# First mixer: products of one chain in runs on TensorE, the modulation's four at a time, low halves of weights by VectorE

## The chip, the cores and the metric

The kernel runs on one core of a Trainium2 chip. The time is the device time of one execution in microseconds (us). TensorE (PE) multiplies matrices, VectorE (DVE) and ScalarE (ACT) work on elements, GpSimd (POOL) does some of the same more slowly, and SyncE (SP) issues the transfers from memory.

## The reference, cut to what matters

Two blocks of two layers each run on 256 tokens of width 1024 in float32. Only the first layer of the first block (its "mixer") and one small vector for the second block bear on this case:

```python
h = rmsnorm(x, g)
proj = h @ even_w_in                       # 1024 x 3592
y_a = rwkv7_group(h, dh, proj[..., :1536], ...)   # 8 heads of 64
y_b = gdn_group(proj[..., 1536:], ...)            # 4 heads of 128
x = x + concat([y_a, y_b]) @ even_w_out
...
mod_l = silu(c) @ w_ada[layer] + b_ada[layer]     # 1024 x 6144, for block two
mod_c = silu(c_ctx) @ w_ada[layer] + b_ada[layer]
```

`rwkv7_group` and `gdn_group` are recurrences over the 256 tokens.

## The kernel before, in words

**Dense products.** A weight piece (128x1024 floats) is loaded by SP into `raw`. ACT copies it, rounded, into `hi`; `split_w` then forms `lo = raw - hi` (the *low half*). TensorE does three products per 128x128 tile: hi with the activation's high and low halves, lo with the high half (`mm3`; the products read `act,hi`, `act,hi`, `act,lo`). Outside the first mixer DVE forms `lo`. In the first mixer `k.weng` is GpSimd, except for the first chunk of `w_ein`. Three `hi` and three `lo` buffers rotate.

**Chains.** The recurrences are done in chunks of 64 tokens by *units*: `rwkv_unit` (four, each for two heads) and `gdn_unit` (two, each for two heads). Two units run side by side (q = 0: rwkv 0 and 1; q = 1: rwkv 2 and 3; q = 2: both gdn), each in its own buffers (a *lane*). A unit is a long chain of small products, each followed by a copy or an elementwise step on ACT or DVE that the next needs: a prelude on DVE (norms of the keys, decays), the inverse of a triangular matrix (`triangular_inverse`: ten dependent groups of 64x64 products, `Tg,Aa`, `Pg,Tt` and so on), a loop over four chunks that carries the state S (`S,WT`, `tm`, `U,tm`), the outputs (`Rr,tm`, `Rr,U`, `AR,S`) and a norm.

**The modulation** (`ada`): the vector `sv` times 1024x6144 weights, 24 MB in all, in 12 chunks of 512 columns. Of a chunk, eight products of 128 rows x 512 columns go to four strips of 32 columns of the array, four to the first start and four that add to them; ACT copies the sum out (`adat`), TensorE transposes it four times (`ct,adat`), and DVE adds it up (`adas`, `mod`). It shares TensorE with the mixer and is needed only in block two.

**Order.** Every engine works through its own list in order. A scheduler makes the lists before the run, from the dependences and from priorities that the code sets: `k.at(p)` and `k.spread` place dense work between the priorities of the chains, and `ada` gets a chunk every 65 steps. So dense products, modulation and chains are interleaved on TensorE, and the transfers of `raw` and `adaraw` on SP. A transfer whose buffer isn't free holds up those behind it on SP. The helpers give one line to many operations: L374 is every product, L377 every transpose by TensorE, L361 every ACT step, L364, L368 and L371 elementwise steps, L1454 the modulation's products.

Of the kernel before, what the change touches and what calls it, by code (L numbers as in the profile page):

```python
# [10 lines left out]
F32 = mybir.dt.float32  # L11
# [4 lines left out]
ALU = mybir.AluOpType  # L16
# [3 lines left out]
P = 128  # L20
# [8 lines left out]
def pack_w(w, kt, nc):  # L29

    K, N = w.shape
    a = w.reshape(K // (P * kt), kt, P, N // nc, nc)
    return np.ascontiguousarray(a.transpose(3, 0, 2, 1, 4)).reshape(N // nc, K // (P * kt), P, kt * nc)
# [158 lines left out]
def layout(i):  # L192
    i = {k: np.asarray(v) for k, v in i.items()}
    A = {}
    A["vec"] = vec_table(i)
    A["con"] = const_table(False)
    A["conm"] = const_table(True)
    A["xT"] = np.ascontiguousarray(i["x"][0].T.reshape(KT, P, T).transpose(1, 0, 2))
    A["pT"] = np.ascontiguousarray(i["p"][:, 0].transpose(0, 2, 1).reshape(2, 2, P, T).transpose(0, 2, 1, 3))
    w = i["even_w_in"][0]  # L200
    A["w_ein"] = pack_w(w[:, :3584], 4, 256)
    A["w_bba"] = np.ascontiguousarray(w[:, 3584:].reshape(KT, P, 8).transpose(1, 0, 2))
    A["w_lora"] = pack_w(np.concatenate([i["rwkv_w1"][0], i["rwkv_a1"][0], i["rwkv_g1"][0]], 1), 4, 256)
    A["w_lo2"] = np.ascontiguousarray(np.stack([np.concatenate([i["rwkv_w2"][0], i["rwkv_a2"][0]], 0), i["rwkv_g2"][0]], 1))
    A["w_eout"] = pack_w(i["even_w_out"][0], 4, 256)
    for l in range(2):
        A[f"w_m1{l}"] = pack_w(i["mlp_w1"][l], 4, 256)
        A[f"w_m2{l}"] = pack_w(i["mlp_w2"][l], 4, 256)
        A[f"w_pp{l}"] = pack_w(i["ple_w_proj"][l], 2, 512)
        A[f"w_pg{l}"] = pack_w(i["ple_w_gate"][l], 4, 256)  # L210
        A[f"w_up{l}"] = pack_w(i["w_up_2"][l], 4, 256)
        w = i["w_down_2"][l]
        w = np.concatenate([w, np.zeros((256, D), w.dtype)])
        A[f"w_dn{l}"] = pack_w(w, 4, 256)
    A["w_ada0"] = pack_w(i["w_ada_2"][0], 2, 512)
    A["w_ada1"] = np.ascontiguousarray(i["w_ada_2"][1].T).reshape(48, P, D)
    A["crow"] = np.ascontiguousarray(np.broadcast_to(np.stack([i["c_2"][0], i["c_ctx_2"]]), (P, 2, D)))
    A["w_qkv"] = pack_w(i["attn_w_qkv"][0], 4, 256)
    A["w_ao"] = pack_w(i["attn_w_out"][0], 4, 256)
    A["w_ie"] = pack_w(i["w_in_e_2"][0], 4, 256)  # L220
    A["w_oe"] = pack_w(i["w_out_e_2"][0], 4, 256)
    A["w_io"] = pack_w(i["w_in_o_2"][0], 4, 256)
    A["w_oo"] = pack_w(i["w_out_o_2"][0], 4, 256)
    A["ctxT"] = np.ascontiguousarray(i["ctx_2"][0].T.reshape(KT, P, T).transpose(1, 0, 2))
    A["abias"] = attn_bias(i["attn_rel_bias"][0])
    A["nbias"] = na_bias(i["na_rpb_2"][0])
    A["fwd"], A["inv"], A["hyz"], A["hydec"] = dft_tables()
    A["hyw1"] = i["hy_w1_2"][0]
    A["hyw23"] = np.ascontiguousarray(np.stack([i["hy_w2_2"][0], i["hy_w3_2"][0]], 1))
    A["hyw4"] = i["hy_w4_2"][0]  # L230
    return A
# [41 lines left out]
class K:  # L273
    def __init__(self, nc, tc, A, es):
        self.nc, self.tc, self.A, self.es = nc, tc, A, es
        self.cp = self.pool("const", 1)
        self.wraw = self.pool("wraw", 4)
        self.whi = self.pool("whi", 3)
        self.wlo = self.pool("wlo", 3)
        self.psG = self.pool("psG", 1, PSUM)  # L280
        self.sms = [self.pool(f"small{i}", 2) for i in range(3)]
        self.ap = [self.pool("acts0", 1), None]
        self.modp = self.pool("modp", 1)
        self.pse = None
        self.weng = nc.vector
        self.slots = None
        self.later, self.slow = [], []

    def pool(self, name, bufs, space=None, es=None, side=None):
# [81 lines left out]
        (eng or self.nc.vector).scalar_tensor_tensor(out=out, in0=a, scalar=s, in1=b, op0=op0, op1=op1)  # L371

    def mm(self, out, lhsT, rhs, start=True, stop=True):
        self.nc.tensor.matmul(out=out, lhsT=lhsT, rhs=rhs, start=start, stop=stop)  # L374

    def tr(self, out, in_):
        self.nc.tensor.transpose(out=out, in_=in_, identity=self.ident)  # L377

    def vec(self, name, j=0, n=1):
        o = VEC[name] + j  # L380
# [24 lines left out]
    def split_w(self, raw, n, kt):  # L405
        hi = self.whi.tile([P, 1024], F32R, name="hi")
        lo = self.wlo.tile([P, 1024], F32R, name="lo")
        self.act(hi[:, :n], raw[:, :n])
        self.tt(lo[:, :n], raw[:, :n], hi[:, :n].bitcast(F32), ALU.subtract, eng=self.weng)
        return (hi[:, :n].rearrange("p (k n) -> p k n", k=kt), lo[:, :n].rearrange("p (k n) -> p k n", k=kt))  # L410

    def mm3(self, ps, w, x, first, last):
# [558 lines left out]
def layer0_mixer(k, x, bg, ple):  # L971

    nc, A = k.nc, k.A
    es = ExitStack()
# [14 lines left out]
    lanes = [lane(1), lane(2)]  # L989
# [10 lines left out]
    for c in range(4):  # L1000
        xc = x[:, 2 * c:2 * c + 2]
        for e in range(2):
            j = 2 * c + e
# [15 lines left out]
    rst = big.tile([P, T], F32, name="rst")  # L1019
    nc.gpsimd.memset(rst, 1.0)  # L1020
    nc.gpsimd.memset(rst.rearrange("p (c t) -> p c t", c=4)[:, :, 0:1], 0.0)
    rkv = {}
# [12 lines left out]
    lt = big.tile([P, 2, T], F32, name="lt")  # L1035
# [25 lines left out]

    bg()
    lo2 = []
    weng, k.weng = k.weng, nc.vector
    g = k.trickle(norm(), NPACE0, 1)
    for _ in k.chunk("w_ein", 2, [4, 4], [H], lambda *a: (k.finish(g), evac_rkv(*a))):
        pass
    k.weng = weng
    nc.sync.dma_start(out=k.cm, in_=A["conm"])
    lora()  # L1070
    for i in range(2):
# [8 lines left out]
    kq, raws = {}, {}  # L1080
# [32 lines left out]
    G = None  # L1113
    ya, yo = [], []
    L = UNIT
    for q in range(3):
        p = t0 + q * L
        if q == 0:
            dense((3, 1, 5), evac_rkv, p, p + L * 0.9)
        elif q == 1:  # L1120
            dense((6, 8, 10, 7, 9, 11), evac_gdn, p, p + L)
            k.at(p + L // 2)
            G = gdn_gates(k, gp, H, wbb, rb)
        else:
            dense((12, 13), evac_gdn, p, p + L * 0.5)
            yh, yl = y = k.acts(0)
            for m in range(4):
                k.split_act(yh[:, m, :T], yl[:, m, :T], ya[m])
            with k.spread(p + EO[0] * L, p + EO[1] * L, 16):
                for _ in out_proj1(k, "w_eout", y, x, [(0, 0, 4)]):  # L1130
                    pass
            k.at(p + PL * L)
            for _ in ple.products(lambda: k.psD.tile([P, 2, T], F32, name="psx")):
                pass
        for u in range(2):
            k.at(p + u * OFS)
            k.lane(1 + u)
            if q < 2:
                m = 2 * q + u
                ya.append(rwkv_unit(k, m, rkv[0, m], rkv[1, m], rkv[2, m], lt, lo2, rst, *lanes[u]))  # L1140
            else:
                yo.append(gdn_unit(k, u, G, [kq[2 * u], kq[2 * u + 1]], raws[1, u], raws[2, u], *lanes[u]))
            k.lane(0)
    k.at(t0 + 3 * L)
    for u in range(2):
# [286 lines left out]
def ada(k, l, es, step, ofs=0):  # L1432


    nc = k.nc
    w = k.pool("adaw", 2 if l else 3, es=es, side="right")
    o = k.pool("adao", 1, es=es, side="right")
    mod = k.mods[l]
    sv = o.tile([P, KT, 32], F32, name="sv")
    k.at(k.now + ofs)  # L1440
    p = k.now
    nc.gpsimd.memset(sv, 0.0)
    k.act(sv[:, :, 0], k.vec("c", 0, 8), AF.Silu)
    k.act(sv[:, :, 1], k.vec("cctx", 0, 8), AF.Silu)
    for c in range(12):
        k.tc.cur_priority = p + step * c
        ps = k.psG.tile([P, 512], F32, name="psg")
        for pi in range(4):
            raw = w.tile([P, 2, 512], F32, name="adaraw")
            nc.sync.dma_start(out=raw, in_=k.A[f"w_ada{l}"][c, pi].rearrange("p (j n) -> p j n", j=2))  # L1450
            for j in range(2):
                kk = 2 * pi + j
                q = 32 * (kk % 4)
                nc.tensor.matmul(out=ps[q:q + 32], lhsT=sv[:, kk], rhs=raw[:, j], start=kk < 4, stop=kk >= 4, tile_position=(0, q))  # L1454
        t = o.tile([P, 512], F32, name="adat")
        k.act(t, ps)
        ps = k.psG.tile([P, 4, P], F32, name="psg")
        for m in range(4):
            k.tr(ps[:, m], t[:, m * P:(m + 1) * P])
        a = o.tile([P, 4, 2], F32, name="adas")  # L1460
        nc.vector.tensor_reduce(out=a, in_=ps.rearrange("p m (q r) -> p m r q", q=4)[:, :, 0:2], op=ALU.add, axis=AX.X)
        k.tt(mod[:, 4 * c:4 * c + 4], a, k.vec(f"bada{l}", 4 * c, 4)[:, :, None].to_broadcast([P, 4, 2]), ALU.add)
    for j in (8, 32):
        k.ts(mod[:, j:j + 8], mod[:, j:j + 8], 1.0, ALU.add)
    k.tc.cur_priority = p - ofs
# [748 lines left out]
def program(nc, tc, A, out):  # L2214
    with ExitStack() as es:
        k = K(nc, tc, A, es)
# [4 lines left out]
        k.plep = k.pool("plep", 1, es=es1, side="right")  # L2221
        ple = [Ple(k, l) for l in range(2)]
        with ExitStack() as esa:
            k.weng = nc.gpsimd
            y = layer0_mixer(k, x, lambda: ada(k, 0, esa, STEP, OFS0), ple[0])
            k.weng = nc.vector
        k.banks(3, 4)
        k.ap[1] = k.pool("acts1", 1)
        k.stp = stp = k.pool("stp", 1)
# [46 lines left out]
```

## Time and profile before

| | |
|---|---|
| median of 3 runs | 1981.81 us (1980.93 to 1985.22) |
| the profiled execution | 1984.02 us, span of its instructions 1982.2 us |
| first mixer, from the span's start to the end of its last chain | about 388 us |
| TensorE busy over the span | 1904.9 us (96%) |
| DVE / ACT / GpSimd busy | 1382.6 / 911.6 / 161.3 us |

TensorE counts as busy from a product's start to its modelled end, and products overlap; an isolated product is busy two or three times as long as it holds up the next. So a busy share near 100% does not say that the engine could take nothing more. Times in the profile are from the span's start.

### The profile page before, as it was taken

What the parts mean: (1) busy time and instruction counts of PE and PEld (TensorE: products, weight loads), DVE (VectorE), ACT (ScalarE), POOL (GpSimd) and SP (SyncE); (2) the same over time, 40 slices, a digit from 0 to 9 for tenths busy, and PEclk for the clock granted to TensorE, in tenths of its full rate; (3) what the DMA queues carried; (4) which work ended last, traced back from release to release, by engine and by line L of the source; (5) the groups of instructions that cost most, each with busy time, mean ns of one, the idle gap of its engine ahead of it and who ended that gap; (6) DMA issues with size and microseconds to landing.
All of it is one profiled execution on the core that took longest, in us unless ns stands there. A gap on an engine that the chain in (4) does not pass through costs nothing.

```text
span 1982.2 us, 36281 instructions
## 1 busy us (share of the span) xinstructions
PE 1904.9 (96%) x14540; PEld 1682.0 (85%) x14540; DVE 1382.6 (70%) x2838; ACT 911.6 (46%) x1527; POOL 161.3 (8%) x211
## 2 busy tenths in 40 slices
PE   7999999999999999999999998899999999899998
PEld 4665668899999889999998887678888898788998
DVE  6544627586558878676876789859877578888664
ACT  4313224455446665545465555433213354465443
POOL 3412214100000100000001100000000000200000
PEclk9999978999999999999999999899999999999999
DMA  6544312255655446556422113235774254324553
GB/s 242 205 165 149 97 57 75 67 186 184 194 192 199 154 130 206 185 193 195 154 81 62 44 38 104 90 128 197 239 267 157 86 172 158 107 77 161 189 182 127
DMA packets 84401, 292.14 MB, mean 147 GB/s; under 512 B 9639, under 2 KB 11528, under 8 KB 83976
## 3 DMA queue, kind: packets, MB, share of 16 engines
q1 hardware_dynamic: 84232, 289.82, 44.3%
q8 instruction: 114, 1.87, 0.4%
q14 instruction: 55, 0.45, 0.1%
HBM read 288.73 MB, written 1.05 MB: 146 GB/s over the span
## 4 chain that ended last, share of the span: by engine, by line
PE 81%; DVE 13%; ACT 2%; issue 2%; POOL 1%; DMA 0%; ACTq 0%; SPq 0%; DVEq 0%
PE psx L374 75%; PE psg L1454 3%; DVE lo L364 3%; PE psx L377 2%; PE psg L374 1%; ACT hi L361 1%; POOL qb L364 1%; DVE mt L371 1%; DVE act L371 0%; DVE qx L364 0%; DVE hu L371 0%; ACT act L361 0%; DVE qms L1309 0%; DVE act L364 0%; DVE nt L364 0%
## 5 line engine op out<-in xcount | busy, mean ns | idle before, releaser
L374 PE MATMUL psx<-act,hi 128*128 128x256 f32 (+1 forms) x3872 | 830.2, 309 | 23.4 <-ACT hi L361 11.4
L361 ACT ACTIVATE hi<-raw 128x1024 fp32r<-128x1024 f32 (+1 forms) x440 | 453.6, 1032 | 652.0 <-PE psx L374 459.1
L374 PEld LDWEIGHTS psx<-act,hi 128*128 128x128 f32 x3872 | 633.9, 192 | 92.3 <-issue 32.4
L364 DVE TENSOR_TENSOR lo<-raw,hi 128x1024 fp32r<-128x1024 f32 (+1 forms) x406 | 482.0, 1189 | 265.8 <-ACT hi L361 264.2
L374 PE MATMUL psx<-act,lo 128*128 128x256 f32 (+1 forms) x1936 | 596.4, 308 | 4.1 <-DVE lo L364 3.6
L374 PEld LDWEIGHTS psx<-act,lo 128*128 128x128 f32 x1936 | 371.7, 192 | 42.1 <-issue 18.8
L374 PE MATMUL psx<-hi,act 128*128 128x256 f32 x1280 | 242.2, 289 | 2.7 <-ACT act L361 1.5
L374 PEld LDWEIGHTS psx<-hi,act 128*128 128x128 f32 x1280 | 198.8, 190 | 11.2 <-issue 7.0
L374 PE MATMUL psx<-lo,act 128*128 128x256 f32 x640 | 180.8, 283 | 1.2 <-DVE lo L364 1.2
L374 PE MATMUL psx<-fh,hi 128*128 128x256 f32 (+2 forms) x528 | 162.3, 308 | 4.9 <-DVE xc L371 4.9
L374 PE MATMUL psx<-fh,lo 128*128 128x256 f32 (+2 forms) x528 | 162.4, 308 | 1.3 <-DVE lo L364 1.3
L374 PE MATMUL psx<-fl,hi 128*128 128x256 f32 (+2 forms) x528 | 161.7, 306 | 0.0
L374 PE MATMUL psx<-hh,hi 128*128 128x256 f32 x512 | 142.4, 278 | 0.0
L374 PE MATMUL psx<-hlo,hi 128*128 128x256 f32 x512 | 142.2, 278 | 0.0
L374 PE MATMUL psx<-hh,lo 128*128 128x256 f32 x512 | 142.2, 278 | 0.0
L374 PEld LDWEIGHTS psx<-lo,act 128*128 128x128 f32 x640 | 121.5, 190 | 1.4 <-DVE lo L364 1.4
L374 PEld LDWEIGHTS psx<-fh,hi 128*128 128x128 f32 x528 | 101.3, 192 | 10.9 <-issue 6.0
L374 PEld LDWEIGHTS psx<-fh,lo 128*128 128x128 f32 x528 | 101.3, 192 | 8.0 <-DVE lo L364 2.1
L374 PEld LDWEIGHTS psx<-fl,hi 128*128 128x128 f32 x528 | 101.3, 192 | 4.5
L364 POOL TENSOR_TENSOR lo<-raw,hi 128x1024 fp32r<-128x1024 f32 x34 | 81.4, 2396 | 223.6 <-ACT hi L361 167.7
L1484 DVE CUSTOM_DVE_ANT_0 adat<-adaraw,adac 128x1024 f32<-128x1024 f32 x64 | 78.3, 1223 | 28.1 <-DMA adaraw<-in_w_ada 27.1
L374 PEld LDWEIGHTS psx<-hlo,hi 128*128 128x128 f32 x512 | 96.9, 189 | 0.0
(499 smaller groups left out, 2501.6 us busy)
## 6 DMA issues: line engine op xcount, KB each, us to landing
raw<-in_w_m SPq DMA_DIRECT2D x128, 512.0 KB, 3.4
adaraw<-in_w_ada SPq DMA_DIRECT2D x96, 512.0 KB, 4.2
raw<-in_w_up SPq DMA_DIRECT2D x92, 512.0 KB, 3.3
raw<-in_w_dn SPq DMA_DIRECT2D x48, 512.0 KB, 3.4
raw<-in_w_ein SPq DMA_DIRECT2D x28, 512.0 KB, 4.7
raw<-in_w_ie SPq DMA_DIRECT2D x28, 512.0 KB, 3.4
raw<-in_w_qkv SPq DMA_DIRECT2D x24, 512.0 KB, 3.5
raw<-in_w_io SPq DMA_DIRECT2D x18, 512.0 KB, 3.7
```

The lines of the kernel that those rows point to most:

```text
L361: self.nc.scalar.activation(out=out, in_=in_, func=func, **kw)
L364: (eng or self.nc.vector).tensor_tensor(out=out, in0=a, in1=b, op=op)
L371: (eng or self.nc.vector).scalar_tensor_tensor(out=out, in0=a, scalar=s, in1=b, op0=op0, op1=op1)
L374: self.nc.tensor.matmul(out=out, lhsT=lhsT, rhs=rhs, start=start, stop=stop)
L377: self.nc.tensor.transpose(out=out, in_=in_, identity=self.ident)
L1454: nc.tensor.matmul(out=ps[q:q + 32], lhsT=sv[:, kk], rhs=raw[:, j], start=kk < 4, stop=kk >= 4, tile_position=(0, q))
L1484: nc.vector.tensor_tensor_reduce(out=t, in0=raw, in1=row[:, s], scale=1.0, scalar=0.0, op0=ALU.mult, op1=ALU.add, accum_out=mod[:, j, s:s ...
```

## The change

Five edits, all in the first mixer or in what it shares memory with.

- `mm` and `tr` go through a new `pe`. Inside `with k.chains()` a product that is traced directly behind another one (nothing else traced between them) is ordered behind the first of its run on TensorE and gets priority 0, so that the run's products follow as soon as they can. Both kinds of unit are traced in `chains()`.
- A modulation piece is now 1024 KB instead of 512 KB (`pack_w(..., 4, 512)`), with two buffers in place of three; four products of a piece are a run of `chains()`.
- `lo` is formed by DVE everywhere (`weng` goes).
- `dynamic_dma_scratch_size=1024` gives room in the on-chip memory for the larger pieces.

```diff
-    A["w_ada0"] = pack_w(i["w_ada_2"][0], 2, 512)
+    A["w_ada0"] = pack_w(i["w_ada_2"][0], 4, 512)
...
+    def pe(self, emit):
+
+        if not self.runs:
+            emit()
+            return
+        traced = self.nc.cur_bb.bb.instructions
+        if self.head is not None and traced[-1] is self.last:
+            p = self.now
+            self.at(0)
+            with self.tc.issue_after(self.head):
+                self.last = emit().ins
+            self.at(p)
+        else:
+            self.head = self.last = emit().ins
...
-        self.tt(lo[:, :n], raw[:, :n], hi[:, :n].bitcast(F32), ALU.subtract, eng=self.weng)
+        self.tt(lo[:, :n], raw[:, :n], hi[:, :n].bitcast(F32), ALU.subtract)
...
-    w = k.pool("adaw", 2 if l else 3, es=es, side="right")
+    w = k.pool("adaw", 2, es=es, side="right")
...
-        for pi in range(4):
-            raw = w.tile([P, 2, 512], F32, name="adaraw")
-            nc.sync.dma_start(out=raw, in_=k.A[f"w_ada{l}"][c, pi].rearrange("p (j n) -> p j n", j=2))
-            for j in range(2):
-                kk = 2 * pi + j
-                q = 32 * (kk % 4)
-                nc.tensor.matmul(out=ps[q:q + 32], lhsT=sv[:, kk], rhs=raw[:, j], start=kk < 4, stop=kk >= 4, tile_position=(0, q))
+        for pi in range(2):
+            raw = w.tile([P, 4, 512], F32, name="adaraw")
+            nc.sync.dma_start(out=raw, in_=k.A[f"w_ada{l}"][c, pi].rearrange("p (j n) -> p j n", j=4))
+            with k.chains():
+                for j in range(4):
+                    q = 32 * j
+                    k.pe(lambda: nc.tensor.matmul(out=ps[q:q + 32], lhsT=sv[:, 4 * pi + j], rhs=raw[:, j], start=pi == 0, stop=pi == 1, tile_position=(0, q)))
...
-            k.weng = nc.gpsimd
             y = layer0_mixer(k, x, lambda: ada(k, 0, esa, STEP, OFS0), ple[0])
-            k.weng = nc.vector
...
-    nc = bacc.Bacc("TRN2", target_bir_lowering=False, num_devices=1)
+    nc = bacc.Bacc("TRN2", target_bir_lowering=False, num_devices=1, dynamic_dma_scratch_size=1024)
```

What moves in the engines' lists: over the first mixer the 96 modulation products stand in 69 separate runs before and in 24 runs of four after. The dense products (`act,hi`, `act,lo`, `act,wbh`, `act,wbl`, `ph`, `plo`) stand in 166 stretches between other products before, in 119 after; the chains' products in 130 stretches before, 98 after. On DVE 36 subtractions are added, and on POOL 36 go. From the first layer's MLP on, TensorE's list is the same in both, down to its end (10,963 of 13,197 entries).

TensorE, before, in the opening of the mixer: dense products of `w_ein`, with the modulation's products (`adaraw,sv`) between them.

```order
L1454 MATMUL psg<-adaraw,sv 32x512
L374 MATMUL psx<-act,hi 128x256 x2
L1454 MATMUL psg<-adaraw,sv 32x512
L374 MATMUL psx<-act,lo 128x256
L1454 MATMUL psg<-adaraw,sv 32x512
L374 MATMUL psx<-act,hi 128x256 x2
L1454 MATMUL psg<-adaraw,sv 32x512
L374 MATMUL psx<-act,lo 128x256
L1454 MATMUL psg<-adaraw,sv 32x512
```

Five products of the modulation stand apart there, each between dense ones. After, there are two runs in the same opening, of this form:

```order
L374 MATMUL psx<-act,hi 128x256 x2
L1474 MATMUL psg<-adaraw,sv 32x512 x4
L374 MATMUL psx<-act,lo 128x256
L374 MATMUL psx<-act,hi 128x256 x2
L374 MATMUL psx<-act,lo 128x256
```

TensorE, before, in the triangular inverse of rwkv units 0 and 1: each x16 is one product group of both lanes (eight blocks each).

```order
L374 MATMUL psx<-Tg,Aa 64x64 x16
L1454 MATMUL psg<-adaraw,sv 32x512
L374 MATMUL psx<-Pg,Tt 64x64 x16
L1454 MATMUL psg<-adaraw,sv 32x512 x4
L374 MATMUL psx<-Tg,Aa 64x64 x16
L1454 MATMUL psg<-adaraw,sv 32x512
L374 MATMUL psx<-act,lo 128x256
L374 MATMUL psx<-act,hi 128x256 x2
L374 MATMUL psx<-act,lo 128x256
L374 MATMUL psx<-Pg,Tt 64x64 x16
L1454 MATMUL psg<-adaraw,sv 32x512 x2
```

After, the same place:

```order
L374 MATMUL psx<-Tg,Aa 64x64 x16
L374 MATMUL psx<-Pg,Tt 64x64 x16
L374 MATMUL psx<-act,hi 128x256
L374 MATMUL psx<-Tg,Aa 64x64 x8
L374 MATMUL psx<-act,hi 128x256
L1474 MATMUL psg<-adaraw,sv 32x512 x4
L374 MATMUL psx<-Tg,Aa 64x64 x8
L374 MATMUL psx<-Pg,Tt 64x64 x16
L374 MATMUL psx<-act,lo 128x256
L374 MATMUL psx<-Tg,Aa 64x64 x8
```

In the whole of this inverse there were ten runs of the modulation, and one is left. Fewer dense products stand between the groups, and the lanes' blocks of eight come one lane after the other.

DVE, after, while the first norm (`nt`, `rbp`) is computed that the first evacuation (`zsh`) waits for; before, no `lo` stands there:

```order
L368 TENSOR_SCALAR nt<-psx 128x256
L364 TENSOR_TENSOR lo<-raw,hi 128x1024
L368 TENSOR_SCALAR rbp<-nt 128x256
L364 TENSOR_TENSOR lo<-wb,hi 128x1024
L364 TENSOR_TENSOR nt<-rbp 128x256
L364 TENSOR_TENSOR raw<-raw,wb 128x1024
L364 TENSOR_TENSOR nt<-nt 128x256
L371 SCALAR_TENSOR_TENSOR nt<-nt 128x256
L371 SCALAR_TENSOR_TENSOR rbp<-nt,rbp 128x256
L364 TENSOR_TENSOR lo<-raw,hi 128x1024
L364 TENSOR_TENSOR nt<-rbp 128x256
L364 TENSOR_TENSOR lo<-wb,hi 128x1024
```

The four low halves have come from POOL's list into the middle of this norm. Of the 36 that come to DVE, 11 stand ahead of the first unit's DVE steps and 25 among those of the units.

## Rows read from the trace of the kernel before

**Rows 1.** Stretches: length, busy PE, PEld, DVE, ACT, POOL; clock, DMA share, GB/s

```profile
0.00:34.00 34.00, 20.89 (x102) 14.06 (x103) 24.44 (x32) 15.67 (x24) 11.57 (x17) 1.00 0.72 259
34.00:68.00 34.00, 34.00 (x204) 22.14 (x202) 10.10 (x15) 10.62 (x13) 14.71 (x8) 1.00 0.62 219
68.00:175.00 107.00, 100.29 (x944) 65.12 (x947) 56.11 (x149) 30.30 (x63) 24.57 (x22) 0.97 0.47 161
175.00:302.00 127.00, 123.01 (x979) 79.49 (x972) 58.37 (x169) 38.30 (x77) 24.79 (x20) 0.87 0.29 94
302.00:388.00 86.00, 82.17 (x901) 74.28 (x900) 56.37 (x145) 38.46 (x65) 30.43 (x19) 0.96 0.21 69
139.00:151.00 12.00, 12.00 (x127) 9.18 (x127) 6.71 (x19) 1.44 (x6) 2.44 (x3) 1.00 0.19 63
247.00:272.00 25.00, 25.00 (x91) 17.09 (x90) 5.26 (x22) 9.37 (x19) 3.63 (x2) 0.52 0.12 43
```

**Rows 2.** Waits on the chain that ended last, 0 to 388 us

```profile
by line: PE psx L374 52.6%; PE psg L1454 15.1%; issue 5.0%; PE psx L377 1.7%; DVE nt L364 1.4%; DMA adaraw<-in_w_ada 1.4%; DVE nrs L371 1.3%; PE psg L377 1.3%; DVE mod L364 1.2%; ACT act L361 1.1%; DVE dsh L371 1.0%; ACT hi L361 1.0%; DVE r
...
20.82 2.09 DVE raw L364
...
30.34 0.43 DVE nt L371
...
292.90 2.06 DVE ntm L364
```

**Rows 3.** Groups of instructions, 0 to 388 us

```profile
L1454 PE MATMUL psg<-adaraw,sv 128*32 128x512 f32 x192 | 76.2, 616 | 1.9 <-DMA adaraw<-in_w_ada 1.9
...
L364 POOL TENSOR_TENSOR lo<-raw,hi 128x1024 fp32r<-128x1024 f32 x34 | 81.4, 2396 | 223.6 <-ACT hi L361 167.7 <-PE psx L374 29.4 <-ACT Pg L361 26.4
...
L364 DVE TENSOR_TENSOR lo<-raw,hi 128x1024 fp32r<-128x1024 f32 x4 | 4.9, 1220 | 1.0 <-ACT hi L361 1.0
```

**Rows 4.** TensorE in order of time, in the opening: start, length, products

```profile
35.00 0.40 PE L374 MATMUL psx<-act,hi 128*128 128x256 f32 x2
35.24 0.28 PE L374 MATMUL psx<-act,lo 128*128 128x256 f32 x1
...
42.94 0.28 PE L374 MATMUL psx<-act,hi 128*128 128x256 f32 x1
43.15 1.04 PE L1454 MATMUL psg<-adaraw,sv 128*32 128x512 f32 x2
44.12 0.38 PE L374 MATMUL psx<-act,hi 128*128 128x256 f32 x1
44.44 1.04 PE L1454 MATMUL psg<-adaraw,sv 128*32 128x512 f32 x2
```

**Rows 5.** TensorE in order of time, in the two rwkv inverses

```profile
112.22 1.20 PE L374 MATMUL psx<-Tg,Aa 64*64 64x64 f32 x32
...
115.45 1.06 PE L1454 MATMUL psg<-adaraw,sv 128*32 128x512 f32 x8
116.44 1.20 PE L374 MATMUL psx<-Tg,Aa 64*64 64x64 f32 x32
...
138.59 0.66 PE L377 MATMUL psg<-ct,adat 128*128 128x128 f32 x4
...
232.27 1.20 PE L374 MATMUL psx<-Tg,Aa 64*64 64x64 f32 x32
...
241.37 1.25 PE L374 MATMUL psx<-Tt,Pg 64*64 64x64 f32 x32
```

**Rows 6.** Stretches as in rows 1, the modulation's products (L1454) alone: PE, PEld

```profile
34.00:68.00 34.00, 12.59 (x36) 1.69 (x36) 1.00 0.62 219
```

**Rows 7.** POOL and DVE in order of time, 139 to 142 us

```profile
139.51 2.36 POOL L364 TENSOR_TENSOR lo<-raw,hi 128x1024 fp32r<-128x1024 f32 x1 [15.20 <-PE psx L374]
139.55 2.33 DVE L364 TENSOR_TENSOR mod<-adas,vt 128x8 f32<-128x8 f32 x1
...
```

**Rows 8.** What SP's queue waited for, 0 to 388 us: total, times, longest

```profile
SPq L1450 <- PE psg L1454: 142.6, 35, 16.0
```

More of the change, by code (lines that the diff above doesn't have):

```diff
@@ L284, in __init__ @@
         self.pse = None
-        self.weng = nc.vector
         self.slots = None
+        self.runs, self.head = False, None
         self.later, self.slow = [], []
@@ L373, in mm, with chains @@
     def mm(self, out, lhsT, rhs, start=True, stop=True):
-        self.nc.tensor.matmul(out=out, lhsT=lhsT, rhs=rhs, start=start, stop=stop)
+        self.pe(lambda: self.nc.tensor.matmul(out=out, lhsT=lhsT, rhs=rhs, start=start, stop=stop))
     def tr(self, out, in_):
-        self.nc.tensor.transpose(out=out, in_=in_, identity=self.ident)
+        self.pe(lambda: self.nc.tensor.transpose(out=out, in_=in_, identity=self.ident))
+    def pe(self, emit):
[11 more added lines that the diff above has]
+            self.head = self.last = emit().ins
+    @contextmanager
+    def chains(self):
+        self.runs = True
+        yield
+        self.runs, self.head = False, None
     def vec(self, name, j=0, n=1):
@@ L1063, in layer0_mixer @@
     lo2 = []
-    weng, k.weng = k.weng, nc.vector
     g = k.trickle(norm(), NPACE0, 1)
@@ L1067, in layer0_mixer @@
         pass
-    k.weng = weng
     nc.sync.dma_start(out=k.cm, in_=A["conm"])
@@ L1137, in layer0_mixer @@
             k.lane(1 + u)
[L1138 to L1142, printed above, removed]
+            with k.chains():
+                if q < 2:
+                    m = 2 * q + u
+                    ya.append(rwkv_unit(k, m, rkv[0, m], rkv[1, m], rkv[2, m], lt, lo2, rst, *lanes[u]))
+                else:
+                    yo.append(gdn_unit(k, u, G, [kq[2 * u], kq[2 * u + 1]], raws[1, u], raws[2, u], *lanes[u]))
             k.lane(0)
@@ L1447, in ada @@
         ps = k.psG.tile([P, 512], F32, name="psg")
-        for pi in range(4):
-            raw = w.tile([P, 2, 512], F32, name="adaraw")
-            nc.sync.dma_start(out=raw, in_=k.A[f"w_ada{l}"][c, pi].rearrange("p (j n) -> p j n", j=2))
-            for j in range(2):
-                kk = 2 * pi + j
-                q = 32 * (kk % 4)
-                nc.tensor.matmul(out=ps[q:q + 32], lhsT=sv[:, kk], rhs=raw[:, j], start=kk < 4, stop=kk >= 4, tile_position=(0, q))
+        for pi in range(2):
+            raw = w.tile([P, 4, 512], F32, name="adaraw")
+            nc.sync.dma_start(out=raw, in_=k.A[f"w_ada{l}"][c, pi].rearrange("p (j n) -> p j n", j=4))
+            with k.chains():
+                for j in range(4):
+                    q = 32 * j
+                    k.pe(lambda: nc.tensor.matmul(out=ps[q:q + 32], lhsT=sv[:, 4 * pi + j], rhs=raw[:, j], start=pi == 0, stop=pi == 1, tile_position=(0, q)))
         t = o.tile([P, 512], F32, name="adat")
```

## The prediction

> **What bounds the kernel now.** I read the changed lists first: from the first MLP on, TensorE's list is the same in both kernels, so everything happens in the first mixer, the first 388 us of the span. Then the busy time by stage [rows 1]. TensorE is nominally full in every stage after the first, but the clearest sign is elsewhere: in 34 to 68 us it takes 34.00 of 34 us while DVE has 10.10 and ACT 10.62. In the unit stages (68 to 175, 175 to 302, 302 to 388) DVE is at 52, 46 and 66%. So TensorE is contended, and no other engine is full. Third, the chain of waits over the mixer [rows 2]: 52.6% of it are TensorE's other products, 15.1% the modulation's, which is 0.151 × 388 = 58.6 us. The groups of instructions [rows 3] give the modulation 76.2 us of TensorE in all (two records per product, so 192 for 96). About 77% of its time is therefore on the path: the mixer waits for a vector that nobody needs before block two.
>
> **What a modulation run costs.** One product alone holds TensorE from 43.15 to 44.12, 0.97 us [rows 4]. Four that follow each other (the x8 row) hold it from 115.45 to 116.44, 0.99 us [rows 5]: they lie in different strips of 32 columns and run at the same time. The price is per run, not per product. 69 runs took 76.2 us, 1.10 each, a few of them at the lower clock. 24 runs of four at 1.0 take 24 us. TensorE is freed of 52 us; the part on the path shrinks from 58.6 to 0.77 × 24 = 18.5. **Term 1: -40 us.** Bounds: -52 if all of it was in the way; -17 if it counts only where I can see it directly. That is, first, an inverse: ten dependent products took 26.4 us (112.22 to 138.59) with ten runs among them, but five took 9.1 us (232.27 to 241.37) with none [rows 5]; at that pace ten take 18.2, so the first inverse gives 8 us. Second, 34 to 68 us, where TensorE alone is full: the modulation has 12.59 us there for 18 products [rows 6]; the same products in runs of four take 4.5, and 8 go.
>
> The Trainium skill speaks for less here: in "TensorE: Matmul & The Clock Gate", Part 3, a packing of three column strips (M=32, N=512) is listed with a speedup of 2.38, not 3. An estimate by that share gives a run of four about 1.24 us, 24 runs 30 us, and a gain some 4 us smaller. The x8 row, 0.99 us against 0.97, decides for the full factor of four, and I keep it.
>
> **Fewer changes of shape.** Two dense products hold TensorE from 35.00 to 35.24, 0.12 each; one dense product between two modulation runs holds it from 44.12 to 44.44, 0.32; one ahead of a run 0.21 (42.94 to 43.15) [rows 4]. Every entry from dense work into tiled work thus costs 0.1 to 0.2 us beside the products. The dense stretches fall from 166 to 119: 47 × 0.2 = 9.4, of which 0.77 on the path. **Term 2: -7 us** (0 to -9; 0 if the chains, not TensorE, set the pace there).
>
> **Low halves from POOL to DVE.** POOL took 2.40 us for one, DVE takes 1.22 [rows 3]. While POOL does one, DVE can stand: `mod`, 128x8 elements, took 2.33 us from 139.55, beside a POOL subtraction of 2.36 from 139.51 [rows 7]. On the chain of waits there are eleven DVE pieces of 2.06 to 2.90 us, the first at 20.82, the last at 292.90, where a step of 128x256 at 30.34 takes 0.43 [rows 2]. Taken together about 20 us of the path are such standing, and it ends. In exchange DVE gets 36 × 1.22 = 44 us. Eleven come ahead of the units: most of these fall where DVE has 10.10 of 34 us busy [rows 1] and cost nothing there (without that cover, up to 13 us). 25 stand among the units' steps, 30.5 us. A subtraction delays a chain when it stands in front of a step that is ready; I take DVE's busy share over 68 to 388, (56.11 + 58.37 + 56.37) / 320 = 53%, as the share that does: 16 us. **Term 3: -4 us** (-20 if all hide in DVE's waits; +10 if all 25 lie on the path).
>
> **Coarser transfers.** Two buffers of 1024 KB replace three of 512 KB, in the same 24 MB. SP already stood 142.6 us in 35 waits with a modulation load at its head [rows 8], 4.1 us each, and weight loads behind it. There are now 24 loads and the lists put several runs in close pairs, so both buffers come free together and 2 MB have to land before the next pair. In the opening 34 × (259 + 219) = 16.25 MB landed by 68 us [rows 1]; at 259 GB/s that needs 62.7 us, whereas terms 1 and 2 would put that point at about 58. **Term 4: +4 us** (0 to +12; the upper end if every second pair waits 2 us).
>
> **The clock.** From 247 to 272 us the granted share was 0.52, nearly all at 1.2 GHz, and the state loop that took 12 us in 139 to 151 at a share of 1.00 took 25 [rows 1]. Ahead of the drop TensorE had the small products of an inverse with a few dense ones between [rows 5]. In the new lists the first inverse looks more like that, with one or two dense products between the groups in place of modulation. A drop could come in another stage (+13) or two (+26), or that one could go (-13). **Term 5: +2 us.**
>
> The rest is free: the larger `adaw` pool and the smaller scratch are room only, and `adat`'s copies, transposes and sums are as many as before. POOL, which loses 36 subtractions, keeps its fills, `Dm`, `yn`, `kb` and `kd`; nothing waits on it more than now.
>
> **Sum.** -40 - 7 - 4 + 4 + 2 = -45 us. The profiled execution took 1984.0 us, so 1939.0; it lay 2.2 us above the median of the three runs, which gives **1937 us**. The gain should be spread as some 10 us in the opening, 15 to 20 in each rwkv stage and little in the gdn stage, where there is no modulation.
>
> **The rivals.**
> *Chains take over.* The freed TensorE time turns into idle: a product's successor waits for ACT and DVE anyway. For it: the eleven long DVE pieces and the 5.0% of the path that nothing explains. Against: only 58.6 of 76.2 us need be on the path for term 1, and the two inverses show the difference directly. Term 1 falls to its lower bound, -17, which makes the sum -22: 1960, or 1973 with one more clock drop.
>
> *More than that.* Nearly all of TensorE's 52 + 9 us is returned and the long half-speed stretch goes as well: 1981.8 - 61 - 13 + 4 = 1912; anything below 1920 counts here.
>
> *DVE's list blocks the chains: slower.* A low half in DVE's list waits until ACT has made `hi`, and ACT for its load; on POOL that wait cost nobody anything, and it was 167.7 us in all [rows 3]. On DVE, every chain step listed behind it stands too. Without term 3 the other terms give 41 us, with the 20 of standing 61; 25 subtractions use that up at 2.4 us each, their own 1.22 included. If they take 3.2 us on average, the time is 1981.8 - 61 + 80 = 2001. Against: POOL's waits were long because it had nothing else to do, and the list puts few subtractions inside the inverses. The Trainium skill ("TensorE: Matmul & The Clock Gate", Architectural detail) calls ACT's and DVE's queues strict first-in first-out, which is this rival's premise; no row here shows how long such waits on DVE would be.
>
> *The change doesn't do what it says.* The four products of a run wait one by one, or late 1 MB pieces hold TensorE for as long as the runs save: within 4 us of 1982. Against: one piece holds all four operands.
>
> **How the numbers follow.** My forecast, a gain of 25 to 62 us (1920 to 1957): 0.62. More: 0.12. Chains take over or clock drops (1957 to 1978): 0.15. No change: 0.04. Slower: 0.07. A measurement here tells 0.2%, 4 us, from no change. So faster 0.89, same 0.04, slower 0.07. The range 1908 to 1966 leaves out the slower and unchanged cases, some 0.07 of the smaller gains and 0.03 below. The forecast's own range is 1920 to 1957.
>
> **What the changed profile would show.** Right: the modulation's products at 24 to 27 us busy and under 7% of the mixer's chain of waits; no DVE piece of 128x256 above 2 us; the first inverse at 18 to 21 us; the last `og` transposes near 338 us instead of 383; nothing different after the mixer but its start. Wrong: TensorE idle ahead of chain products, released by DVE, with a `lo` just ahead on DVE; waits of TensorE for `adaraw`; a granted share below 0.8 in the first rwkv stage; POOL-like long pieces on DVE still there. A gain near 20 us would mean that term 1's share of the path was wrong, one near 70 that the chains had waited for TensorE nearly always.

## The result and the profile after

| | before | after |
|---|---|---|
| median | 1981.37 us (1977.54 to 1985.22, 4 runs) | 1896.94 us (1895.3 to 1898.74, 4 runs) |
| the profiled execution | 1984.02 us | 1898.16 us, span 1896.2 us |
| granted clock over the span | 0.977 | 0.985 |

The ratio is 0.9563, with an interval of 0.953 to 0.9597. The change gains about 87 us. 45 were forecast, and the time lies below the range. Of the 85.9 us between the two profiled executions, 82.5 are gone by the end of the first mixer: its last `og` transpose starts at 301.4 us instead of 383.9.

The mixer in stages of after (length, busy PE, PEld, DVE, ACT, POOL; clock, DMA share, GB/s), to be laid beside [rows 1]. The last two rows are most of the state loops of the two rwkv stages.

```profile
0.00:54.00 54.00, 40.91 (x305) 34.12 (x305) 34.34 (x58) 25.68 (x38) 1.24 (x15) 1.00 0.83 309
54.00:124.00 70.00, 69.81 (x868) 52.05 (x868) 46.92 (x143) 24.94 (x54) 5.73 (x13) 1.00 0.52 195
124.00:201.00 77.00, 76.54 (x923) 58.12 (x922) 52.03 (x157) 31.18 (x63) 5.54 (x11) 1.00 0.45 163
201.00:304.00 103.00, 100.73 (x1032) 89.58 (x1030) 70.83 (x184) 50.03 (x84) 7.68 (x11) 0.93 0.24 78
101.00:109.00 8.00, 8.00 (x61) 5.99 (x59) 4.38 (x16) 1.06 (x1) 0.00 (x0) 1.00 0.01 3
178.00:188.00 10.00, 10.00 (x87) 8.02 (x87) 4.45 (x15) 1.63 (x3) 0.00 (x0) 1.00 0.17 52
```

By the first and last instructions of each stage, the opening shrinks from 68.0 to 54.0 us, the first rwkv stage from 105.5 to 69.8, the second from 128.3 to 77.0, and the gdn stage grows from 82.1 to 100.7. POOL's column is nearly empty, and the 1.2 GHz stretch of the second rwkv stage is gone. From its first `S,WT` product to its last, the state loop of the second rwkv stage took 22.7 us before; after it takes 10.1, at a share of 1.00. (Only part of that is the clock, as term 5 below shows.)

The chain of waits of after, 0 to 304 us: first the shares by line (as [rows 2]), then every low half of DVE on it.

```profile
by line: PE psx L374 72.2%; PE psg L1474 6.6%; DVE lo L364 3.0%; DMA adaraw<-in_w_ada 2.4%; PE psx L377 2.1%; PE psg L377 1.9%; issue 1.4%; ACT act L361 1.3%; DMA x<-in_xT 1.2%; ACT hi L361 1.0%; DVE kbe L364 0.5%; ACT Pg L361 0.5%; DVE Tt 
...
10.98 1.24 DVE lo L364
...
20.95 1.13 DVE lo L364
...
22.29 1.13 DVE lo L364
...
26.14 1.19 DVE lo L364
...
37.84 1.23 DVE lo L364
...
39.51 7.30 DMA adaraw<-in_w_ada
...
245.88 1.98 DVE lo L364
249.53 1.13 DVE lo L364
```

TensorE's products are now 72.2% of the path instead of 52.6%, and the modulation is down from 15.1% to 6.6%. Of DVE's 39 low halves (37 from `raw`, two from `wb`) seven are on the path, 9.0 us in all: five in the opening (5.9 us; the first of them was DVE's before, too) and two among the units (3.1 us). One wait for a modulation load stands out, 7.30 us at 39.51.

Groups of after over the same stretch (busy, mean ns | idle before), to be laid beside [rows 3]:

```profile
L364 DVE TENSOR_TENSOR lo<-raw,hi 128x1024 fp32r<-128x1024 f32 x37 | 45.9, 1242 | 13.8 <-ACT hi L361 5.4 <-PE psx L374 5.2 <-DMA strm<-in_ctxT 2.7
...
L1474 PE MATMUL psg<-adaraw,sv 128*32 128x512 f32 x192 | 25.6, 604 | 0.4 <-DMA adaraw<-in_w_ada 0.4
```

The modulation takes 25.6 us instead of 76.2. SP's waits with a modulation load at its head, in the view of waits [rows 8]:

```profile
SPq L1470 <- PE psg L1474: 48.2, 15, 8.7
```

TensorE of after in order of time, the first inverse: first, one of the modulation's runs in it, and last rows (as [rows 5]).

```profile
82.31 1.15 PE L374 MATMUL psx<-Tg,Aa 64*64 64x64 f32 x32
83.47 1.15 PE L374 MATMUL psx<-Pg,Tt 64*64 64x64 f32 x32
...
85.79 1.07 PE L1474 MATMUL psg<-adaraw,sv 128*32 128x512 f32 x8
86.79 0.68 PE L374 MATMUL psx<-Tg,Aa 64*64 64x64 f32 x16
...
96.54 1.33 PE L374 MATMUL psx<-Tt,Pg 64*64 64x64 f32 x32
97.80 0.39 PE L374 MATMUL psx<-act,hi 128*128 128x256 f32 x1
```

The ten dependent product groups take 15.5 us (82.31 to 97.80), against 26.4 before.

### The profile page after: what moved, and what is told of

Same layout as the page of the kernel before. It is cut to its first block, busy times and chain, and to the rows that moved or that the text cites. A ratio compares the mean times of both kernels' runs of the same rounds, so it can differ in the third digit from the quotient of the medians.

```text
span 1896.2 us, 36237 instructions
## 1 busy us (share of the span) xinstructions
PE 1831.4 (97%) x14540; PEld 1660.7 (88%) x14540; DVE 1383.3 (73%) x2874; ACT 911.2 (48%) x1526; POOL 75.4 (4%) x175
## 4 chain that ended last, share of the span: by engine, by line
PE 86%; DVE 9%; ACT 2%; issue 1%; POOL 1%; DMA 1%; SPq 0%; ACTq 0%; DVEq 0%
PE psx L374 81%; DVE lo L364 3%; PE psx L377 2%; PE psg L1474 1%; PE psg L374 1%; ACT hi L361 1%; POOL qb L364 1%; DVE qx L364 0%; DVE mt L371 0%; DMA adaraw<-in_w_ada 0%; ACT act L361 0%; DVE act L371 0%; DVE act L364 0%; PE psg L377 0%; DVE qms L1329 0%
## 5 line engine op out<-in xcount | busy, mean ns | idle before, releaser
L374 PE MATMUL psx<-act,hi 128*128 128x256 f32 (+1 forms) x3872 | 821.0, 307 | 24.4 <-ACT hi L361 11.0
L364 DVE TENSOR_TENSOR lo<-raw,hi 128x1024 fp32r<-128x1024 f32 (+1 forms) x440 | 524.4, 1194 | 283.1 <-ACT hi L361 273.3
L374 PEld LDWEIGHTS psx<-hh,hi 128*128 128x128 f32 x512 | 96.1, 188 | 0.0
L374 PEld LDWEIGHTS psx<-hh,lo 128*128 128x128 f32 x512 | 96.1, 188 | 0.0
```

Source lines behind the costliest of these rows:

```text
L364: (eng or self.nc.vector).tensor_tensor(out=out, in0=a, in1=b, op=op)
L374: self.pe(lambda: self.nc.tensor.matmul(out=out, lhsT=lhsT, rhs=rhs, start=start, stop=stop))
```

## The experiments

The change has three parts that can be switched apart: the modulation's runs of four, the low halves on DVE, and the runs inside the units. The first three kernels do one part alone, three others leave one out. Each line below gives the median of the kernel and of the kernel before beside it; a gain is given by the ratio. The scheduler makes the lists anew for each kernel, so none of them differs from another in its edit alone: the modulation, not touched in e2 and e5, stands in 69 runs before, 66 in e2 and 59 in e5. `dynamic_dma_scratch_size` is changed in e1, e3 and e5 as well, and no run has that edit by itself.

**e1, the modulation alone.** Before, with `pe`, the 1 MB pieces and `chains()` around a piece; the units are not in `chains()`.

```diff
-    w = k.pool("adaw", 2 if l else 3, es=es, side="right")
+    w = k.pool("adaw", 2, es=es, side="right")
...
+            with k.chains():
+                for j in range(4):
```

> The kernel before with the modulation's edit alone: 1 MB pieces, runs of four (24 runs instead of 69), the low halves still on POOL, no runs in the units. Theory A (the modulation's hold on TensorE was the larger half of the 85 us, and nearly all of its 52 us came back): 50 us faster, about 1932. Theory B (the rest came because DVE no longer stands beside POOL, and so TensorE is fed steadily and keeps its clock; the modulation gave no more than the 40 us of the prediction's first term): 30 to 40 us faster, about 1945, with half-speed stretches of 40 us or more left in the first 388 us.

1945.76 us (1944.28 to 1958.72) against 1986.47; ratio 0.9808 [0.9757, 0.9859], about 38 us. Its second state loop ran at 1.2 GHz even longer than before's did:

```profile
210.00:254.00 44.00, 44.00 (x197) 30.26 (x196) 9.37 (x34) 12.32 (x25) 2.44 (x2) 0.50 0.13 42
```

**e2, the low halves alone.** Before, without GpSimd for `lo`.

```diff
-            k.weng = nc.gpsimd
             y = layer0_mixer(k, x, lambda: ada(k, 0, esa, STEP, OFS0), ple[0])
-            k.weng = nc.vector
```

> The kernel before with the low halves by DVE and nothing else. Theory A: within 8 us of before, as the prediction's third term (-4) has it. Theory B: 25 to 40 us faster, about 1950, since the eleven long DVE pieces on the chain of waits go and half-speed stretches with them.

1955.86 us (1949.73 to 1957.88) against 1986.47; ratio 0.984 [0.9796, 0.9883], about 32 us where the prediction gave this part 4.

**e3, the runs in the units alone.**

```diff
-            if q < 2:
+            with k.chains():
+                if q < 2:
```

> The kernel before with runs in the units alone (rwkv_unit and gdn_unit inside chains()), modulation and low halves as before. Both theories: a small gain, 5 to 12 us (the prediction's second term, -7); over 20 us would be a third cause that neither has: that a chain's products standing together shorten the chains themselves.

1967.49 us (1964.67 to 1970.75) against 1986.47; ratio 0.9899 [0.9849, 0.9948], about 20 us. The three single gains sum to 90 us, about what all of them give together (87).

**e4, no modulation at all.** Before, without the modulation's loads, products, copies, transposes and sums; the vector for block two is a constant.

```diff
-    for c in range(12):
...
+    nc.gpsimd.memset(mod, 0.1)
```

> The kernel before without the modulation of block two's first layer: its loads, products, copies, transposes and sums are left out and its result is filled with a constant. It bounds what the modulation costs in all. By its share of the chain of waits 59 us come back (about 1922), by its busy time with the transposes 85. Theory A: 70 us or more. Theory B: 45 to 60.

1930.6 us (1923.02 to 1935.49) against 1986.47; ratio 0.9714 [0.9666, 0.9762], about 57 us. That is what the whole modulation cost by itself. Theory A falls: e1 with 38 us, e2 with 32 and e4 with 57 all lie where theory B put them. e3 lies above the 5 to 12 us that both had, near the 20 from which a third cause was to be looked for.

**e5, both engines.** What makes e2 worth 32 us? Either DVE no longer stands beside POOL's subtractions (theory S), or `lo` is there earlier, since DVE forms it in 1.2 us and POOL in 2.4 (theory L). Here DVE forms `lo`, and POOL does the same 36 subtractions into a tile that nobody reads.

```diff
-        self.tt(lo[:, :n], raw[:, :n], hi[:, :n].bitcast(F32), ALU.subtract, eng=self.weng)
+        self.tt(lo[:, :n], raw[:, :n], hi[:, :n].bitcast(F32), ALU.subtract)
+        if self.weng is self.nc.gpsimd:
+            self.tt(self.spare[:, :n], raw[:, :n], hi[:, :n].bitcast(F32), ALU.subtract, eng=self.weng)
```

> The kernel before with the low halves by DVE, as in the DVE-only run, and POOL still doing its 36 subtractions of the same operands, into a tile that nobody reads. Theory S (DVE stands while POOL subtracts; that standing was the cost): the 30 us of the DVE-only run are gone, the time is that of before or up to 20 us more. Theory L (the low half is ready 1.2 us earlier after hi, and that was the gain): 20 us or more faster than before still.

1986.94 us (1982.25 to 1990.54, 10 runs) against 1983.52; ratio 1.0005 [0.9974, 1.0036]. All of e2's gain is lost again, so L falls. Groups of e5's mixer, then the same of e2, and last the sum `mod` in the mixer of before:

```profile
L364 POOL TENSOR_TENSOR spare<-raw,hi 128x1024 f32<-128x1024 f32 x34 | 94.9, 2791 | 165.1 <-ACT hi L361 98.1 <-issue 55.6 <-DVE x L364 9.5
L364 DVE TENSOR_TENSOR lo<-raw,hi 128x1024 fp32r<-128x1024 f32 x39 | 60.8, 1560 | 31.6 <-ACT hi L361 31.6
...
L368 DVE TENSOR_SCALAR dsh<-zsh,vt 128x256 f32<-128x256 f32 x12 | 6.0, 525 | 0.0
L364 DVE TENSOR_TENSOR mod<-adas,vt 128x8 f32<-128x8 f32 x12 | 6.0, 497 | 0.1
```

```profile
L364 DVE TENSOR_TENSOR lo<-raw,hi 128x1024 fp32r<-128x1024 f32 x39 | 47.4, 1221 | 32.8 <-ACT hi L361 22.1 <-ACT Z L361 4.0 <-ACT Pg L361 2.9
...
L368 DVE TENSOR_SCALAR dsh<-zsh,vt 128x256 f32<-128x256 f32 x12 | 4.5, 387 | 0.0
L364 DVE TENSOR_TENSOR mod<-adas,vt 128x8 f32<-128x8 f32 x12 | 1.9, 162 | 0.1
```

```profile
L364 DVE TENSOR_TENSOR mod<-adas,vt 128x8 f32<-128x8 f32 x12 | 10.5, 878 | 0.2
```

With POOL at work DVE's own subtraction takes 1560 ns instead of 1221, and the 128x8 sum 497 instead of 162. POOL also holds `raw` and `hi` longer in e5 than in e2, and the lists differ; neither is separated in the 31 us between them.

**e6, e7, e8: after with one part undone.** e6 forms `lo` on POOL again, e7 has the old modulation, e8 no runs in the units.

```diff
+            k.weng = nc.gpsimd
             y = layer0_mixer(k, x, lambda: ada(k, 0, esa, STEP, OFS0), ple[0])
+            k.weng = nc.vector
```

```diff
-    A["w_ada0"] = pack_w(i["w_ada_2"][0], 4, 512)
+    A["w_ada0"] = pack_w(i["w_ada_2"][0], 2, 512)
...
-    w = k.pool("adaw", 2, es=es, side="right")
+    w = k.pool("adaw", 2 if l else 3, es=es, side="right")
```

```diff
-            with k.chains():
+            if True:
                 if q < 2:
```

> The changed kernel with the low halves on POOL again, as before; modulation in runs and runs in the units stay. If the three edits add up: 1897 + 31 = 1928. If they share one pool of freed time: at most 15 us above the changed kernel, 1912. Theory S also expects long DVE pieces of 2 us and more back on the chain of waits.

> The changed kernel with the modulation as before: 512 KB pieces, three buffers, no runs of four. If the edits add up: 1897 + 39 = 1936. If they share the freed time: 1915 or less.

> The changed kernel without runs in the units; modulation in runs and low halves by DVE stay. If the edits add up: 1897 + 19 = 1916. If they share the freed time: within 8 us of the changed kernel, 1897 to 1905.

Against 1983.52: e6 1933.64 us (ratio 0.9744 [0.9685, 0.9804]), e7 1944.47 (0.9801 [0.9741, 0.9861]), e8 1916.81 (0.9664 [0.9597, 0.973]). Taken from after's 1896.94, the low halves are worth 37 us there, the modulation 48, the unit runs 20. So the gains don't share one pool of freed time, which would have put e6 at 1912 or less and e7 at 1915 or less. In e6 theory S expected long DVE pieces back on the chain of waits, and they are: eleven single pieces of 2.10 to 2.49 us, where after's path has no DVE piece of 2 us or more. First the shares of e6's path, then three of the pieces:

```profile
by line: PE psx L375 56.6%; PE psg L1477 6.1%; DVE dsh L372 5.3%; PE psx L378 2.6%; issue 2.2%; DMA raw<-in_w_ein 1.9%; DVE nt L365 1.7%; PE psg L378 1.6%; DVE bt L365 1.3%; DVE dsh L369 1.1%; DVE zsh L365 1.0%; DVE tmp L369 0.9%; DVE ntm L
...
20.66 2.37 DVE raw L365
...
188.33 2.29 DVE dsh L372
...
315.16 2.25 DVE oms L372
```

e8, without the unit runs, has the 1.2 GHz stretch in its second state loop again:

```profile
198.00:222.00 24.00, 24.00 (x143) 19.64 (x135) 6.16 (x22) 7.55 (x18) 0.10 (x1) 0.51 0.11 33
```

**e9, big pieces without runs of four.** After, with `chains()` around a piece taken away.

```diff
-            with k.chains():
+            if True:
                 for j in range(4):
```

> The changed kernel with 1 MB modulation pieces, but without runs of four: the four products of a piece are placed singly (67 runs in the list, as in the kernel before). Theory: only the runs matter, the piece size nothing, so this is as slow as with the old modulation (1944): 1937 to 1950. If the larger pieces gave part of the gain: 1930 or less.

1945.25 us (1940.0 to 1954.32) against 1984.82; ratio 0.9795 [0.9758, 0.9832], the time of e7. Without runs of four, the size of the pieces is worth nothing either way. Its modulation, in the groups of its mixer:

```profile
L1474 PE MATMUL psg<-adaraw,sv 128*32 128x512 f32 x192 | 70.2, 605 | 0.0
```

**e10, e11, e12: the gdn stage.** Why is it 19 us longer in after? Runs in the gdn units might hold dense products back (theory G; e10 takes those runs out), or too much dense work is left for the last stage (theory D; e11 puts one chunk a stage earlier, e12 shortens the planned stage from 320 steps to 260).

```diff
+            if q < 2:
+                with k.chains():
...
+            else:
+                if True:
```

```diff
-            dense((3, 1, 5), evac_rkv, p, p + L * 0.9)
+            dense((3, 1, 5), evac_rkv, p, p + L * 0.7)
+            dense((6,), evac_gdn, p + L * 0.7, p + L * 0.95)
...
-            dense((6, 8, 10, 7, 9, 11), evac_gdn, p, p + L)
+            dense((8, 10, 7, 9, 11), evac_gdn, p, p + L)
```

```diff
-UNIT = 320
+UNIT = 260
```

> The changed kernel with runs in the four rwkv units and none in the two gdn units. The gdn stage was 18 us longer in the changed kernel's trace than before. Theory D (dense work that the faster rwkv units ran ahead of is done there, 175 dense products instead of 78 between the last rwkv product and the first gdn product): within 6 us of the changed kernel, 1892 to 1903. Theory G (the runs themselves hold up the gdn units): 10 us or more faster, 1887 or less.

> The changed kernel with one of the six dense chunks of the second unit stage (chunk 6) given priorities in the first, so that 103 instead of 175 dense products are left between the last rwkv product and the first gdn product. Theory D: TensorE is idle or waits in the first rwkv stage often enough to take part of these 72 products (8.6 us at 0.12): 3 to 9 us faster, about 1891. If TensorE is the bound in every stage alike: within 3 us of the changed kernel.

> The changed kernel with UNIT at 260 instead of 320, the distance in priorities between the unit stages, so that dense work stands closer in the stages (145 dense products left between the last rwkv product and the first gdn product). Theory D: 0 to 5 us faster. If TensorE is the bound in every stage alike: within 3 us of the changed kernel.

Against 1984.82: e10 1907.74 us (1906.92 to 1908.59; ratio 0.96 [0.9571, 0.9629]), e11 1896.96 (0.9549 [0.9522, 0.9576]), e12 1899.61 (0.9557 [0.953, 0.9584]). G falls: without their runs the gdn units are slower, and only they. The stages of e10 are those of after up to 201 us, and the last is 11 us longer:

```profile
54.00:124.00 70.00, 69.80 (x868) 52.03 (x868) 46.88 (x143) 24.95 (x54) 5.73 (x13) 1.00 0.52 196
124.00:201.00 77.00, 76.28 (x920) 57.91 (x919) 51.84 (x156) 31.19 (x63) 5.48 (x11) 1.00 0.45 164
201.00:315.00 114.00, 106.94 (x1044) 93.16 (x1044) 76.42 (x190) 56.22 (x91) 6.75 (x12) 0.93 0.25 83
```

D falls too. e11 does move the work: its stages, in place of after's 70, 77 and 103 us, are

```profile
54.00:133.00 79.00, 78.09 (x910) 58.66 (x910) 49.72 (x148) 26.43 (x55) 6.03 (x13) 1.00 0.50 180
133.00:221.00 88.00, 87.31 (x1006) 66.04 (x1005) 58.67 (x174) 43.42 (x79) 7.69 (x13) 1.00 0.42 154
221.00:304.00 83.00, 78.33 (x910) 70.53 (x908) 62.45 (x164) 41.97 (x74) 7.70 (x10) 1.00 0.25 84
```

and the end is the same. TensorE is busy for 94 to 99% of each of these stages, and the work moved between them changes their lengths but not their sum. That is the rival both expectations named, TensorE as the bound in every stage alike. The gdn stage of after is longer because it holds the work that the faster rwkv stages left: between the last rwkv product and the first gdn product stand 175 dense products, where before there were 78. No version tried beats after.

## Why the prediction was wrong

**The clock has a price, and it can be taken out, as an estimate.** TensorE runs at 2.4 or 1.2 GHz, so its time at half speed in a run is 2 × (1 − granted share) × span. The kernel before ran 28 times. Its fastest run, 1975.18 us, had a share of 0.983, which is 67 us at half speed; its longest, 2003.94, had 0.965, 140 us. That is 28.8 us for 73, 0.39 us for each us at half speed, and a line through all 28 gives the same 0.39, with 1.3 us of scatter about it. The price fits the runs of the other kernels too: e8's four lie 15 us apart, and 3.4 once it is taken off. That it also holds from one kernel to the next, where the slow stretches lie elsewhere, is assumed. With it each kernel's difference from the 1984.2 us of before (median of the 28, 97 us at half speed) parts into the clock and the rest. Medians of four runs (ten for e5); I take each figure as uncertain by some 3 us.

| kernel | parts in it | at half speed, us | difference, us | by the clock | rest |
|---|---|---|---|---|---|
| e1 | modulation | 109 | -38 | +5 | -43 |
| e2 | low halves | 68 | -28 | -11 | -17 |
| e3 | unit runs | 81 | -17 | -7 | -10 |
| e6 | modulation, unit runs | 83 | -51 | -5 | -45 |
| e7 | low halves, unit runs | 54 | -40 | -17 | -23 |
| e8 | modulation, low halves | 88 | -67 | -4 | -64 |
| after | all three | 55 | -87 | -16 | -71 |
| e4 | no modulation work | 129 | -54 | +13 | -66 |
| e5 | e2, and POOL subtracts too | 107 | +3 | +4 | -1 |

The rests of the single parts add up: -43 - 17 - 10 = -70, and all three together have -71. Part of that is luck, for the pairs don't quite: modulation and unit runs have 8 us less together (-45) than alone, and the low halves have -13 beside the unit runs, -21 beside the modulation and -26 beside both. Beside the prediction's own sum:

**Term 1 (-40) was right.** The part measures -43 by the table, -35 to -48 when taken with the others. Both numbers it rests on held: 24 runs take 25.6 us (24 forecast) and 6.6% of the path (under 7% forecast). e4's rest, -66, is 23 us more than e1's; that is what a modulation in runs of four still costs with its loads, copies, transposes and sums, where 18.5 were forecast for the products. e9 shows that the runs do it and not the pieces. The rival "chains take over", which put this term at -17, falls with it. By the three-strip figure of the Trainium skill ("TensorE: Matmul & The Clock Gate", Part 3) the prediction estimated about 30 us of TensorE; the trace shows 25.6.

**Term 2 (-7) was about right net of the clock.** Runs in the units give -10 alone, and -2 to -7 beside other parts. That this is the price of changes of shape is not shown: no run tells it from products of a chain simply standing closer together.

**Term 3 (-4) failed, at the step that took DVE's busy share for the share of low halves on the path.** What failed is the 16 us charged, 25 subtractions × 1.22 × 53%. After's chain of waits holds two of these 25, 3.1 us, and four of the eleven in the opening, 4.7 us, where the prediction had put nothing. In e2, the low halves alone, the path holds three of all 36, 3.5 us:

```profile
31.20 1.14 DVE lo L364
...
287.53 1.22 DVE lo L364
...
351.23 1.13 DVE lo L364
```

The other side of the term, 20 us of DVE standing beside POOL, was close: 20 - 3.5 is 16.5, and e2's rest is 17. e5 against e2 says the same less directly: 31 us, of which 15 by the clock (39 us more at half speed) and 16 left for DVE, buffers and lists. But the standing has no fixed price. Beside the other two parts the low halves are worth 26. A likely reason is in e6's path, where TensorE's products are in the way less: `dsh` steps alone are 5.3% of it, 17 us, against 1.0% of before's, 4 us [rows 2]. DVE is busy half the time, but 52.6 + 15.1% of before's path are products of TensorE. Where a step of DVE is late by 1.2 us, TensorE mostly has other work queued ahead of its successor; that is my reading, and no run isolates it. The rival "DVE's list blocks the chains" needed 2.4 us for each of the 25. DVE did stand for `hi` ahead of its low halves, 22.1 us in e2 and 5.4 in after, where POOL waited 167.7 before; but only the three low halves above came to e2's path.

**Term 4 (+4) cost little or nothing.** The wait it feared is there once, 7.30 us at 39.51 (2.4% of the path), but before's path had one as well (1.4%, [rows 2]):

```profile
97.98 5.34 DMA adaraw<-in_w_ada
```

SP's waits with a modulation load at their head fell from 142.6 to 48.2 us. No run has runs of four with the small pieces, so the term isn't measured by itself.

**Term 5 (+2) failed in sign.** It set a fall in one or two more stages against the loss of the one that was there. The table's estimate is -16: half-speed time falls from 97 to 55 us, and the long stretch of [rows 1] is gone. The modulation edit alone pushed it the way that was forecast (109 us, the 44 us stretch of e1). The other two parts, which the term did not weigh, pulled it down: 68 us in e2, 81 in e3. Its unit was too large as well. It took 13 us for one fall, from a state loop of 25 us against one of 12. By its `S,WT` products the second loop of before ran from 256.4 to 279.1, 22.7 us. In e2 the same loop took 17.8 us at full clock, in e8 12.1 at half, in after 10.1 at full. First e2's loop, then e8's, and last the modulation's products in e2's loop alone:

```profile
236.70:254.80 18.10, 18.10 (x96) 9.48 (x96) 6.17 (x25) 9.12 (x18) 0.10 (x1) 1.00 0.26 81
199.10:211.50 12.40, 12.40 (x52) 9.66 (x48) 4.72 (x18) 4.20 (x11) 0.10 (x1) 0.50 0.21 63
236.70:254.80 18.10, 6.39 (x15) 0.83 (x14) 1.00 0.26 81
```

So the other work inside the loop counts as well as the clock: in e2 six runs of the modulation stand in it, 6.39 us, and in e8 and after none.

So by this estimate, of the 42 us missed 13 are term 3, 18 the clock, 4 term 4, and the rest two small excesses of terms 1 and 2. The rival "more than that" was right that the long stretch goes, and wrong on where the rest would come from: it wanted nearly all 61 us of TensorE back, and modulation and unit runs gave 53 one by one and 45 together. What it lacked are the low halves.

**Where the gain lay** was forecast as 10 us in the opening, 15 to 20 in each rwkv stage, little in the gdn stage. It was 14, 36, 51 and -19: the rwkv stages ran ahead of the dense work, which then filled the gdn stage. The first inverse came out at 15.5 us where 18 to 21 were forecast.

**Open.** Why the clock falls in the second state loop of before (25 us at 0.52), of e1 (44 at 0.50) and of e8 (24 at 0.51), and has no long fall there in any kernel with runs in the units, stays open. That is no more than a correlation: e2 and e5 have no unit runs and no such fall either (1.00 in both loops). And what of the 31 us between e5 and e2 comes from POOL holding buffers, or from other lists, isn't separated.

## What to carry to other kernels

Charge a step that is moved to another engine by what that engine has on the chain of waits, not by its busy share: DVE at 53% hid all but two of the 25 steps added among the units, in a kernel whose path before was two thirds TensorE. When a change has separable parts, price each one's side effects on the engine that it leaves as well; here leaving POOL was worth more than the work brought to DVE cost. And before crediting a gain, take the clock out with a price from the kernel's own runs; by that estimate about a fifth of this gain was granted clock.

## What the runs showed of the hardware

- While POOL subtracts, DVE's steps can take many times as long. A DVE sum of 128x8 took 878 ns on average in before's mixer, where POOL forms the low halves, and 162 in e2's. The Trainium skill ("SBUF — State Buffer", SBUF: two separate sides) says that a DVE step with two inputs in the on-chip memory and a POOL step that reads there need the same port pair, and that the first of them holds it to its end while the other stands; the trace agrees, 2.33 us beside 2.36 [rows 7]. 36 such subtractions, 100 us of POOL in e5, went with 31 us more than e2's 1956, of which an estimated 15 are clock.
- Time at half speed cost 0.39 us for each us (28 runs of before, 1975 to 2004 us), in a kernel where TensorE is busy 96% of the span. What hides the rest isn't shown.
- Edits that regroup the same work, or move 36 subtractions between engines, took the half-speed time of the whole program from 97 us to anything between 54 (e7) and 109 us (e1).
